# Other start addresses for matmul operands, another passage into the FFN, and twelve placements of FFN up's weights

## The chip, the core and the metric

The kernel runs on one core of one Trainium2 chip. The metric is device time in microseconds for one execution of the whole layer. The work of the five engines is named as the profile names it: PE is TensorE's matmuls and PEld its weight loads, DVE is VectorE, ACT is ScalarE, POOL is GpSimd, and SP is SyncE, which here only issues DMAs.

## What is computed

One layer of a diffusion backbone for 256 latent tokens and 256 context tokens of width 2048, all in fp32. Two token mixers (windowed attention with shared keys, neighbourhood attention) run in parallel, are gated, merged and projected; then comes a gated FFN with a short convolution:

```python
h = modulate(rms_norm(x, g_attn_pre), sh1, sc1)
hc = modulate(rms_norm(ctx, g_attn_pre), csh1, csc1)
# mixer: q, k, v, gates from h @ w_in (keys and values from hc too)
y = (sigmoid(ga) * (oa @ w_br_a) + sigmoid(gb) * (ob @ w_br_b)) @ w_o
x = x + gt1 * rms_norm(y, g_attn_post)

h = modulate(rms_norm(x, g_ffn_pre), sh2, sc2)
u = depthwise_conv(h @ w_up, conv_w, conv_b)       # 2048 -> 2 x 5632
a, g = split(u, 2)
x = x + gt2 * rms_norm((silu(g) * a) @ w_down, g_ffn_post)
```

The shifts, scales and gates come from `silu(c) @ w_mod + b_mod`.

## The kernel before

**Three matmuls for one product.** TensorE multiplies in a reduced form of fp32 here (`F32R`). So every operand is split in two parts, a high one (a rounded copy, made by ScalarE) and a low one (the rest, made by VectorE), in `split` (L114). A product is high x high + low x high + high x low; the low x low part is left out.

**Weights in blocks.** The weights `ws` come as 222 blocks of 128 x 2048 fp32 (1 MB), in the order in which they are used: values (10 blocks), queries (16), gates and branches (48), output projection (16), FFN up (88), FFN down (44); the constants `B_V` ... `B_DN` number the first of each. `raw_block` (L104) has SP load a block into one of four buffers `raw`; `halves` (L125) splits it in two halves of 1024 columns into the tiles `wh` and `wl` (two buffers each); `block` (L152) hands out the next one, has the one after it split, and loads some blocks ahead. The keys have units of their own (`ku`), in the buffers of `wh`.

**Two ways to use a block.** A matmul has a stationary operand, loaded by its weight load, and a moving one that streams past it.

- In the values (tile `pv`, L585), the output projection (`py_o`) and FFN down (`py_d`, both L800), the activations are stationary and the weights move, 512 columns at a time (the last part of the values: 256). Three matmuls make one product.
- In the queries (`pq`), gates (`pg`), branches (`pb`) and FFN up (`pu`), `mm2` (L159) has the weights stationary and the activations moving. The activations' high and low parts lie side by side, so one matmul with 512 columns does high and low against the high weights, and one with 256 columns does the low weights: a pair.
- The keys (`pk`, L387) have the weights stationary and 256 moving columns; the scores (`s`, L681) have 512 columns and run in runs of up to six within the queries.

**Where operands start.** SBUF tiles lie one after another, in the order in which pools and tiles are made, each rounded up to 32 bytes. In the built program this gives, in bytes past a multiple of 64 (every slice that a matmul takes starts at a multiple of 512 within its tile):

| Stage | stationary | moving |
|---|---|---|
| keys `pk` | weights 32 | activations 0 |
| values `pv` | activations 0 | weights 32 |
| queries `pq`, gates `pg` | weights 32 | activations 0 |
| scores `s` | queries 0 | keys 0 |
| branches `pb` | weights 32 | attention output 32 |
| output projection `py_o` | gated sum 32 | weights 32 |
| FFN up `pu` | weights 32 | activations 0 |
| FFN down `py_d` | gated FFN 32 | weights 32 |

**The passage into the FFN.** `norm_gain` (L787) does the output projection in four column groups. In the last, the last three blocks are done for the first 128 tokens (t = 0) and then for the other 128 (t = 1), so that the norm of the first half can run beside the matmuls of the second. `close` (L804) squares a half on ScalarE and multiplies by the gain on VectorE; `residual` (L870) takes the root (`rstd_tok`, L834), adds to x (`x1`, four steps of 512 columns), squares the sum for the next norm and takes its root. FFN up's first block is split in between, behind the first half's close (L832), its two pieces queued behind a step of `residual` (L879). `scaled` (L886) multiplies both halves by their scale, half of the column groups on ScalarE. Then 33 filler matmuls (`keep_busy`, L899), and 32 transposes (`ptx`, L905), whose output in PSUM is read by VectorE or ScalarE into a temporary `h2t` (L912, L914), by ScalarE into the high part of `h2` (L915), and from both VectorE makes the low part (L916). FFN up's matmuls follow as pieces of `h2` come.

A scheduler sets each engine's order from the program's order, the dependencies and its costs; `issue_after` queues an instruction behind another one on its engine. All engines work through their queues in order.

## Time and profile before

| | us |
|---|---|
| median of 3 runs | 1532.22 (1531.57 to 1532.34) |
| the profiled execution | 1532.26 |
| its span, first to last instruction | 1530.5 |

The granted clock of TensorE over the span is 0.999. By stage, from the first to the last matmul that writes the stage's tile:

| Stage | from | to |
|---|---|---|
| keys `pk` | 10.3 | 163.8 |
| values `pv` | 158.0 | 275.2 |
| queries and attention `pq`, `s`, `po` | 275.0 | 440.5 |
| gates and branches `pg`, `pb` | 440.4 | 691.4 |
| output projection `py_o` | 691.2 | 780.8 |
| transposes `ptx` | 787.7 | 796.9 |
| FFN up `pu` | 791.6 | 1281.2 |
| FFN down `py_d` | 1281.0 | 1522.9 |

A row of the profile's groups reads: line, engine, operation, output <- inputs (buffer numbers left out), shape, count, then busy time and mean duration of one, then the engine's idle time before it and what ended that. A row of the timeline begins with the start and the duration in microseconds. A matmul's duration includes its filling and draining, which overlap with its neighbours'; how far apart two matmuls start is read from their starts.

### The profile page before, as it was taken

To read this page: it belongs to the slowest core of one execution; us is meant where nothing else is said; L and a number is where in the kernel's file an instruction comes from. 1 tells how busy PE (TensorE), PEld (TensorE's weight loads), DVE (VectorE), ACT (ScalarE), POOL (GpSimd) and SP (SyncE) were. 2 spreads that over 40 slices of the span, in tenths; PEclk is the share of its full clock that TensorE was granted. 3 is DMA by queue.
4 is the path that set the end of the run, shared out by engine and by line. 5 is a ranking of instruction groups with operands and counts; after the bars stand their busy time and mean duration, and the time that the engine had idled before them with its cause. 6 is when DMAs were issued, how large, how long until landed. Compare 5 with 4: busy or idle time off the path is not lost.

```text
span 1530.5 us, 22661 instructions
## 1 busy us (share of the span) xinstructions
PE 1512.7 (99%) x9062; PEld 1319.4 (86%) x9062; DVE 1131.6 (74%) x1670; ACT 784.7 (51%) x1277; POOL 1.7 (0%) x10
## 2 busy tenths in 40 slices
PE   8999999999999999999999999999999999999998
PEld 8988888899988888888888888888888888888886
DVE  3478798888888989887768887888788776444444
ACT  4332533676774445454467555555555555344342
POOL 0000000000000000000000000000000000000000
PEclk9999999999999999999999999999999999999999
DMA  9978778634458888888955666666666556555552
GB/s 348 385 269 330 287 287 330 256 111 131 139 199 332 320 325 330 336 321 318 376 203 202 248 226 242 245 233 223 242 242 240 198 193 248 220 192 193 192 192 83
DMA packets 59113, 382.19 MB, mean 250 GB/s; under 512 B 6528, under 2 KB 6912, under 8 KB 16768
## 3 DMA queue, kind: packets, MB, share of 16 engines
q1 hardware_dynamic: 58288, 379.68, 67.1%
q8 instruction: 71, 1.16, 0.3%
q10 hardware_dynamic: 720, 1.07, 0.2%
q14 instruction: 34, 0.28, 0.0%
HBM read 376.48 MB, written 4.24 MB: 249 GB/s over the span
## 4 chain that ended last, share of the span: by engine, by line
PE 96%; DVE 1%; ACT 1%; DMA 1%; issue 1%; DVEq 0%; ACTq 0%
PE pu L164 21%; PE py_d L800 16%; PE pu L165 11%; PE pv L585 7%; PE pg L164 7%; PE pk L387 6%; PE py_o L800 5%; PE pq L164 4%; PE pb L164 4%; PE pg L165 4%; PE pq L165 2%; PE pb L165 2%; PE po L711 2%; PE s L681 1%; PE pm L295 1%; PE pt L702 1%
## 5 line engine op out<-in xcount | busy, mean ns | idle before, releaser
L122 DVE TENSOR_TENSOR wl<-raw,wh 128x1024 fp32r<-128x1024 f32 x444 | 529.7, 1221 | 236.7 <-ACT wh L118 236.3
L118 ACT ACTIVATE wh<-raw 128x1024 fp32r<-128x1024 f32 x444 | 453.1, 1054 | 300.8 <-PE py_d L800 131.3
L164 PE MATMUL pu<-h,wh 128*128 128x512 f32 x1408 | 488.6, 390 | 0.1
L165 PE MATMUL pu<-h,wl 128*128 128x256 f32 x1408 | 397.0, 282 | 0.0
L164 PEld LDWEIGHTS pu<-h,wh 128*128 128x128 f32 x1408 | 264.4, 188 | 55.8 <-DVE h L916 0.3
L165 PEld LDWEIGHTS pu<-h,wl 128*128 128x128 f32 x1408 | 266.1, 189 | 0.0
L800 PE MATMUL py_d<-wh,ff 128*128 128x512 f32 x704 | 218.1, 391 | 0.0
L164 PE MATMUL pg<-hx,wh 128*128 128x512 f32 x464 | 161.5, 390 | 0.0
L800 PEld LDWEIGHTS py_d<-wh,ff 128*128 128x128 f32 x704 | 132.2, 188 | 27.9
L194 DVE SCALAR_TENSOR_TENSOR raw<-raw,crb 128x2048 f32<-128x2048 f32 x64 | 146.1, 2285 | 3.8 <-DMA raw<-in_wm_b_dram 3.1
L800 PE MATMUL py_d<-wl,ff 128*128 128x512 f32 x352 | 138.0, 392 | 0.0
L165 PE MATMUL pg<-hx,wl 128*128 128x256 f32 x464 | 130.8, 282 | 0.0
L387 PE MATMUL pk<-hx,ku 128*128 128x256 f32 x480 | 117.0, 286 | 1.8 <-DVE kT L453 1.7
L387 PE MATMUL pk<-hc,ku 128*128 128x256 f32 x480 | 114.1, 280 | 0.0
L169 ACT ACTIVATE half_u<-pu 128x256 f32<-128x256 f32 x88 | 33.5, 383 | 152.8 <-PE pu L165 152.8
L164 PE MATMUL pq<-hx,wh 128*128 128x512 f32 x304 | 108.2, 395 | 0.0
L164 PEld LDWEIGHTS pg<-hx,wh 128*128 128x128 f32 x464 | 87.1, 188 | 18.4
L387 PEld LDWEIGHTS pk<-hx,ku 128*128 128x128 f32 x480 | 90.2, 188 | 6.8 <-issue 4.5
L387 PEld LDWEIGHTS pk<-hc,ku 128*128 128x128 f32 x480 | 90.4, 188 | 0.7 <-issue 0.2
L164 PE MATMUL pb<-oab,wh 128*128 128x512 f32 x256 | 90.5, 394 | 0.0
L165 PEld LDWEIGHTS pg<-hx,wl 128*128 128x128 f32 x464 | 87.7, 189 | 0.0
L165 PE MATMUL pq<-hx,wl 128*128 128x256 f32 x304 | 85.5, 281 | 0.0
(181 smaller groups left out, 1942.5 us busy)
## 6 DMA issues: line engine op xcount, KB each, us to landing
raw<-in_ws_dram SPq DMA_DIRECT2D x222, 1024.0 KB, 4.9
raw<-in_wm_b_dram SPq DMA_DIRECT2D x64, 1024.0 KB, 5.1
raw<-in_wm_sc_dram SPq DMA_DIRECT2D x15, 1024.0 KB, 8.2
raw<-in_wm_sh_dram SPq DMA_DIRECT2D x16, 768.0 KB, 7.2
raw<-in_wkt_dram SPq DMA_DIRECT2D x10, 1024.0 KB, 5.2
crb<-sild SPq DMA_DIRECT2D x6, 1024.0 KB, 7.1
raw<-in_wk_dram SPq DMA_DIRECT2D x7, 768.0 KB, 9.0
sd<-in_wm_sd_dram SPq DMA_DIRECT2D x4, 1024.0 KB, 8.8
```

Source lines behind the costliest of these rows:

```text
L118: a_ = nc.scalar.activation(hi, src, AF.Copy)
L122: v_ = nc.vector.tensor_tensor(out=lo, in0=src, in1=hi, op=ALU.subtract)
L164: nc.tensor.matmul(pt[:, :], wh[:, w], a, start=first and i == 0, stop=False, skip_group_check=True)
L165: nc.tensor.matmul(pt[:, :S], wl[:, w], a[:, 0], start=False, stop=last and i == n - 1, skip_group_check=True)
L169: a_ = nc.scalar.activation(t[:], pt[:, S:], AF.Copy)
L194: nc.vector.scalar_tensor_tensor(out=r, in0=r, scalar=1.0, in1=row, op0=ALU.mult, op1=ALU.mult, accum_out=modx[:, j : j + 1])
L295: nc.tensor.matmul(pm[32 * j : 32 * j + 32, t * P : t * P + P], cc[:, q, :], rsc[k + t][:, q * P : q * P + P], start=q < 4, stop=q >= KT - ...
L387: nc.tensor.matmul(pk[:, v * S : v * S + S], wt[:, w], hh[v][:, k, a], start=k == 0 and a == 0 and wt is wh and v == 0, stop=k == KT - 1 a ...
L585: nc.tensor.matmul(pv[i][:, :nw], src[:, k, a, t0 : t0 + P], wt[:, w], start=k == 0 and q == 0, stop=k == KT - 1 and q == 2)
L681: nc.tensor.matmul(s_ps[:], qs[hd][:, a, qt * P : qt * P + P], k_[:], start=q == 0, stop=q == 2)
L711: nc.tensor.matmul(po[:, :S], v_[:, b], pTs[hd][:, b, a], start=b == 0 and q == 0, stop=b == 3 and q == 2)
L800: nc.tensor.matmul(py[t][:], act[:, k, a, t * P : t * P + P], wt[:, w], start=k == 0 and q == 0, stop=k == nk - 1 and q == 2)
```

## The change

It has three parts.

1. **Places.** The small tiles at the start of SBUF change their order and sizes, `cr` and `c2` go into tiles that exist anyway, and the buffers of `wh` and `wl` become 32 elements (128 bytes) longer. All activations now start at 0 bytes past a multiple of 64 (of 128 too), and so do the weights' buffers. Within its buffer a block's high and low part start at an offset, in elements of 4 bytes, that `offset` gives by stage: (0, 0) for values, output projection and FFN down, (8, 8), that is 32 bytes, for queries, gates, branches and the first four blocks of FFN up. The keys' units start at 8 as well.
2. **Twelve placements.** The other 84 blocks of FFN up take the twelve pairs of the table `UP`, seven blocks each.
3. **Passage.** FFN up's first block is split with the blocks before it, ahead of the first half's close. `residual` and `scaled` are rewritten, with another order and share between ScalarE and VectorE; the scalings of column group 3 and one more are ScalarE's. There are 26 fillers in place of 33, and the first piece of `h2` gets a second pair of transposes into a bank of its own (`ptx0b`), which VectorE reads, while ScalarE reads the first one.

The core of the diff:

```diff
+UP = ((0, 8), (8, 0), (4, 4), (0, 4), (4, 0), (4, 8), (8, 4), (12, 12), (2, 2), (16, 16), (8, 24), (24, 8))
...
-    def halves(r, pool=None, after=None):
+    def halves(r, off, pool=None, after=None):
         n = r.shape[-1]
         b = 1 if pool else 2
-        h = (pool or wp).tile([P, 2048], F32R, tag="wh", bufs=b, name=f"wh{nraw[0]}")
-        lo = (pool or wp).tile([P, 2048], F32R, tag="wl", bufs=b, name=f"wl{nraw[0]}")
+        h, lo = (
+            (pool or wp).tile([P, 2048 + 32], F32R, tag=f"w{q}", bufs=b, name=f"w{q}{nraw[0]}")[:, off[i] : off[i] + 2048]
+            for i, q in enumerate("hl"))
...
+    def offset(i):
+
+        if B_UP + 4 <= i < B_DN:
+            return UP[(i - B_UP - 4) // 7]
+        return (0, 0) if i < B_Q or B_WO <= i < B_UP or i >= B_DN else (8, 8)
...
-                parts[q] = halves(raws[q], place.get(q), queue.get(q))
+                parts[q] = halves(raws[q], offset(q - b0), place.get(q), queue.get(q))
...
-                h = wp.tile([P, 2048], F32R, tag="wh", bufs=2, name=f"ku{u}")
+                h = wp.tile([P, 2048 + 32], F32R, tag="wh", bufs=2, name=f"ku{u}")[:, 8 : 8 + 2048]
...
                 for g in range(n - lead, n):
-                    wts.append(block(3, g < n - 1))
+                    wts.append(block(3))
                     part(wts[-1], g, 0)
                 for t in range(2):
...
-                    close(t)
-                    done(t)
-                    if t == 0:
-                        split_to(nblk[0])
+                    close(t, after)
+                    after = done(t)
...
                 a_ = nc.scalar.activation(yg[:, t, cs], x1[:, t, cs], AF.Square, accum_out=ss[:, 1, t, c : c + 1])
-                if t == c == 0:
-                    queue[b0 + B_UP] = (a_.ins, v_.ins)
-            rstd_tok(ss[:, 1, t], r[:, 1, t : t + 1])
-            if t:
-                with tc.issue_after(closed[0]), tc.issue_after(v_.ins):
-                    scaled(0)
-                scaled(1)
...
+            if t == 0:
+                rstd_tok(ss[:, 1, t], r[:, 1, t : t + 1])
+                return a_.ins
+            else:
+                v_ = v_.ins
+                for c in range(3):
+                    with tc.issue_after(v_):
+                        v_ = scaled(0, c)
+                with tc.issue_after(v_):
+                    rstd_tok(ss[:, 1, t], r[:, 1, t : t + 1])
+                scaled(1, 0)
+                a_ = scaled(1, 1)
+                scaled(1, 2)
+                with tc.issue_after(a_):
+                    a_ = scaled(0, 3)
+                with tc.issue_after(a_):
+                    scaled(1, 3)
+                for q in range(2):
+                    sync.dma_start(out=x1d[:, q], in_=x1[:, q])
+
+        def scaled(t, c):
+            cs = slice(c * 512, c * 512 + 512)
+            if c == 3 or (t, c) == (1, 1):
+                return nc.scalar.activation(yg[:, t, cs], x1[:, t, cs], AF.Copy, scale=r[:, 1, t : t + 1]).ins
+            return nc.vector.tensor_scalar(
+                out=yg[:, t, cs], in0=x1[:, t, cs], scalar1=r[:, 1, t : t + 1], scalar2=None, op0=ALU.mult).ins
+
+        norm_gain(zz, KT, yg, grow, ss[:, 0], "o", 2, residual, beside)
         zs.close()
         pu = [acc(f"pu0_{i}") for i in range(4)]
-        keep_busy(33, "2")
+        keep_busy(26, "2")
...
-                    nc.vector.tensor_scalar(out=t_[:], in0=px, scalar1=g_, scalar2=s_, op0=ALU.mult, op1=ALU.add)
+                    nc.vector.tensor_scalar(out=t_[:], in0=px if j else pt0[:, :S], scalar1=g_, scalar2=s_, op0=ALU.mult, op1=ALU.add)
```

Also in it, and not shown: a fourth buffer for the attention's small statistics tile (`st`), and the wider tiles for `r`, `gr` and the warm-up of the root, which only move what lies behind them.

Outside the passage, and a few matmuls of FFN up's first blocks beside it, every engine's instructions stand in the same order as before. In the passage, ScalarE's order from the first half's close on was, before (`py_o3_0` and `py_o3_1` are the two halves' sums, `wh192` is FFN up's first block):

```order
L805 ACTIVATE yg_7006,ss_7008<-py_o3_0_7445 128x512
L838 ACTIVATE r_7009<-ss_7008,r_7009 128x1
L877 ACTIVATE yg_7006,ss_7008<-x1_7005 128x512
L118 ACTIVATE wh192_7551<-raw190_7485 128x1024
L877 ACTIVATE yg_7006,ss_7008<-x1_7005 128x512 x3
L118 ACTIVATE wh192_7551<-raw190_7485 128x1024
L838 ACTIVATE r_7009<-ss_7008,r_7009 128x1
L805 ACTIVATE yg_7006,ss_7008<-py_o3_1_7446 128x512
L838 ACTIVATE r_7009<-ss_7008,r_7009 128x1
L890 ACTIVATE yg_7006<-x1_7005,r_7009 128x512 x2
L877 ACTIVATE yg_7006,ss_7008<-x1_7005 128x512 x4
L838 ACTIVATE r_7009<-ss_7008,r_7009 128x1
```

And in the changed kernel (with its own line numbers; the block is `wh191` there):

```order
L126 ACTIVATE wh191_7534<-raw190_7488 128x1024 x2
L821 ACTIVATE yg_7010,ss_7012<-py_o3_0_7448 128x512
L852 ACTIVATE r_7013<-ss_7012,r_7013 128x1
L891 ACTIVATE yg_7010,ss_7012<-x1_7009 128x512 x4
L821 ACTIVATE yg_7010,ss_7012<-py_o3_1_7449 128x512
L852 ACTIVATE r_7013<-ss_7012,r_7013 128x1 x2
L891 ACTIVATE yg_7010,ss_7012<-x1_7009 128x512 x4
L852 ACTIVATE r_7013<-ss_7012,r_7013 128x1
L915 ACTIVATE yg_7010<-x1_7009,r_7013 128x512 x3
L945 ACTIVATE h2_7005<-ptx0_7657,modx_74,gcol_75 128x256
```

Both pieces of the split moved from between the first half's squares to ahead of its close, and the scalings moved behind the second half's squares.

VectorE, from the second half's gain to the first piece of `h2`, before:

```order
L806 TENSOR_TENSOR yg_7006<-py_o3_1_7446,grow_7007 128x512
L839 RECIPROCAL r_7009<-r_7009 128x1
L874 SCALAR_TENSOR_TENSOR x1_7005<-yg_7006,r_7009,x1_7005 128x512 x4
L892 TENSOR_SCALAR yg_7006<-x1_7005,r_7009 128x512
L836 TENSOR_REDUCE r_7009<-ss_7008 128x1
L892 TENSOR_SCALAR yg_7006<-x1_7005,r_7009 128x512
L837 TENSOR_SCALAR r_7009<-r_7009 128x1
L839 RECIPROCAL r_7009<-r_7009 128x1
L892 TENSOR_SCALAR yg_7006<-x1_7005,r_7009 128x512 x2
L914 TENSOR_SCALAR h2t0_7665<-ptx0_7660,gcol_72,modx_71 128x256
L916 TENSOR_TENSOR h2_7001<-h2t0_7665,h2_7001 128x256
```

And in the changed kernel:

```order
L822 TENSOR_TENSOR yg_7010<-py_o3_1_7449,grow_7011 128x512
L853 RECIPROCAL r_7013<-r_7013 128x1 x2
L888 SCALAR_TENSOR_TENSOR x1_7009<-yg_7010,r_7013,x1_7009 128x512 x4
L916 TENSOR_SCALAR yg_7010<-x1_7009,r_7013 128x512 x3
L850 TENSOR_REDUCE r_7013<-ss_7012 128x1
L851 TENSOR_SCALAR r_7013<-r_7013 128x1
L853 RECIPROCAL r_7013<-r_7013 128x1
L916 TENSOR_SCALAR yg_7010<-x1_7009,r_7013 128x512 x2
L944 TENSOR_SCALAR h2t0_7664<-ptx0b_7656,gcol_75,modx_74 128x256
L946 TENSOR_TENSOR h2_7005<-h2t0_7664,h2_7005 128x256
```

Three scalings of the first half now stand ahead of the second half's reduce, where one stood before, and the first temporary is read from `ptx0b`.

66 lines of the change are left out of this document (32 added, 34 removed).

## The prediction

> **What bounds the kernel now.** I read the busy time on the page first, then the chain that ended last, then the timeline of TensorE inside each stage, and last the timeline around the passage from the output projection to FFN up.
>
> ```profile
> span 1530.5 us, 22661 instructions
> PE 1512.7 (99%) x9062; PEld 1319.4 (86%) x9062; DVE 1131.6 (74%) x1670; ACT 784.7 (51%) x1277; POOL 1.7 (0%) x10
> ...
> PE 96%; DVE 1%; ACT 1%; DMA 1%; issue 1%; DVEq 0%; ACTq 0%
> ```
>
> TensorE is busy for 99% of the span and makes up 96% of the chain. So only two things can move the time: how far apart the matmuls of a stage follow each other (the pitch), and the few places where TensorE waits. Most of the change is about the first, the new passage into FFN up about the second.
>
> A matmul's duration in a row (390 ns and so on) overlaps the next one, so it doesn't give the pitch. The starts do. From five stages, the first and the last row of a steady stretch (the columns are start, duration, engine, line, operation, output<-inputs, shape, count):
>
> ```profile
> 200.28 0.40 PE L585 MATMUL pv<-wl,hx 128*128 128x512 f32 x1
> ...
> 205.88 0.40 PE L585 MATMUL pv<-wl,hx 128*128 128x512 f32 x1
> ```
>
> ```profile
> 1399.61 0.39 PE L800 MATMUL py_d<-wl,ff 128*128 128x512 f32 x1
> ...
> 1402.36 0.39 PE L800 MATMUL py_d<-wl,ff 128*128 128x512 f32 x1
> ```
>
> ```profile
> 340.47 1.09 PE L681 MATMUL s<-k,q 128*128 128x512 f32 x4
> ...
> 395.38 1.54 PE L681 MATMUL s<-k,q 128*128 128x512 f32 x6
> ```
>
> ```profile
> 559.75 0.40 PE L164 MATMUL pb<-oab,wh 128*128 128x512 f32 x1
> ...
> 562.91 0.40 PE L164 MATMUL pg<-hx,wh 128*128 128x512 f32 x1
> ```
>
> ```profile
> 999.78 0.39 PE L164 MATMUL pu<-h,wh 128*128 128x512 f32 x1
> ...
> 1003.94 0.39 PE L164 MATMUL pu<-h,wh 128*128 128x512 f32 x1
> ```
>
> ```profile
> 59.77 0.28 PE L387 MATMUL pk<-hx,ku 128*128 128x256 f32 x1
> ...
> 61.87 0.28 PE L387 MATMUL pk<-hx,ku 128*128 128x256 f32 x1
> ```
>
> The same shape does not cost the same everywhere. With 512 moving columns: pv does 24 matmuls in 5.60 us, 0.2333 each; py_d 12 in 2.75 us, 0.2292; s, two more matmuls in a run cost 1.54 - 1.09 = 0.45 us, so 0.225 to 0.230 within the rounding of the rows, and I use 0.227. A pair of 512 and 256 columns takes 3.16/9 = 0.3511 in pb and 4.16/12 = 0.3467 in pu. The 256-column matmuls of pk follow at 2.10/18 = 0.1167. No row of these stretches has a wait behind it, and the granted clock is 1.00 (in the windows further down), so something about the operands makes the difference.
>
> Set beside the table of places in the section on the kernel, it sorts like this. Where the moving operand starts on a multiple of 64 bytes (s, pu, pk), the pitch is low. Where it starts 32 bytes past one (pv, py_d, pb), it is high, and highest in pv, where the stationary operand does not share that shift. That is a reading of six stages, not a shown cause; every term below that rests on it has a rival.
>
> **The change part by part.** All terms are against the profiled execution's own 1532.26 us (span 1530.5 and 1.76 around it), which is 0.04 above the median of 1532.22.
>
> *Places in FFN down, the output projection and the values.* Counts come from these rows:
>
> ```profile
> L800 PE MATMUL py_d<-wh,ff 128*128 128x512 f32 x704 | 218.1, 391 | 0.0
> L800 PE MATMUL py_d<-wl,ff 128*128 128x512 f32 x352 | 138.0, 392 | 0.0
> L800 PE MATMUL py_o<-wh,zz 128*128 128x512 f32 x256 | 79.0, 392 | 0.0
> L800 PE MATMUL py_o<-wl,zz 128*128 128x512 f32 x128 | 49.6, 393 | 0.0
> L585 PE MATMUL pv<-wh,hx 128*128 128x512 f32 x128 | 40.2, 396 | 0.5 <-ACT wh L118 0.5
> L585 PE MATMUL pv<-wl,hc 128*128 128x512 f32 x64 | 25.3, 395 | 0.0
> ```
>
> After the change both operands of these stages start on a multiple of 64, as in s, which has the same shape and the same rhythm of three matmuls (high by high, low by high, high by low). py_d and py_o together are 1440 matmuls: 1440 x (0.2292 - 0.227) = 3.2 us saved; with s at 0.225 it would be 6.0, with 0.230 a loss of 1.2. pv has two groups of 128 and two of 64, so 384 at 512 columns: 384 x (0.2333 - 0.227) = 2.4 saved (1.3 to 3.2). Its 192 matmuls of 256 columns I leave at nothing; half of pv's difference either way would be 0.6 us.
>
> *Places in the branches.* pb's 256 pairs get an aligned moving operand and a stationary one at 32, which is what pu has: 256 x (0.3511 - 0.3467) = 1.1 us saved. The queries and gates keep the relation that they have now, 32 for the weights and 0 for the activations, so nothing; the first four blocks of FFN up too. VectorE has slack for the faster pace: in the values it is the most loaded, and yet it is idle for a tenth.
>
> ```profile
> 160.00:270.00 110.00, 110.00 (x563) 92.71 (x562) 98.98 (x112) 45.32 (x77) 0.00 (x0) 1.00 0.78 296
> 792.00:1281.00 489.00, 489.00 (x2825) 433.28 (x2824) 388.85 (x579) 286.99 (x459) 0.00 (x0) 1.00 0.63 224
> ```
>
> (The columns after the stretch and its length are busy time and count of PE, PEld, DVE, ACT and POOL, then the granted clock, the DMA share and GB/s.) In the first row VectorE is busy 98.98 of 110 us, and the pace rises by 2.7%; in FFN up it is busy 388.85 of 489, so its splits, 128x1024 each, could take a quarter longer at odd addresses before it became the bound.
>
> *Twelve placements in FFN up.* 84 blocks of 16 pairs, in groups of 7 blocks or 112 pairs. The activations stay aligned. Counted past a multiple of 64, groups 11 and 12 have both parts at 32, as now: nothing. The other ten groups, 1120 pairs, stand at 0, 8, 16 or 48 bytes or in mixtures, which no stage of before shows. Bounds from rows: at the low end a pair made of s's 0.227 and pk's 0.1167, which is 0.3437, so 1120 x 0.0030 = 3.4 us saved; near by on the high side pb's 0.3511, so 1120 x 0.0044 = 4.9 lost; far out, both matmuls paying what pv pays over s, 2 x 0.0063, so 14.1 lost. The nearest rows are pu itself (all the activations' places and some of the weights' stay as they are there) and pb; I take half of pb's surcharge, 2.5 us lost.
>
> *The passage.* The rows around it, from the timeline (in brackets, the idle time before and what ended it), with a row of VectorE's splits from the page (busy time, mean ns) ahead of them:
>
> ```profile
> L122 DVE TENSOR_TENSOR wl<-raw,wh 128x1024 fp32r<-128x1024 f32 x444 | 529.7, 1221 | 236.7 <-ACT wh L118 236.3
> ```
>
> ```profile
> 775.74 0.60 ACT L805 ACTIVATE yg<-py_o 128x512 f32<-128x512 f32 x1 [7.82 <-PE py_o L800]
> 778.68 1.05 ACT L118 ACTIVATE wh<-raw 128x1024 fp32r<-128x1024 f32 x1
> 780.40 0.39 PE L800 MATMUL py_o<-wl,zz 128*128 128x512 f32 x1
> 781.47 1.04 ACT L118 ACTIVATE wh<-raw 128x1024 fp32r<-128x1024 f32 x1
> 782.60 0.57 ACT L805 ACTIVATE yg<-py_o 128x512 f32<-128x512 f32 x1
> 784.53 2.74 DVE L874 SCALAR_TENSOR_TENSOR x<-yg,r,x 128x512 f32<-128x512 f32 x4
> 787.19 0.48 DVE L892 TENSOR_SCALAR yg<-x,r 128x512 f32<-128x512 f32 x1
> 787.72 0.90 PE L905 MATMUL ptx<-ident,yg 128*128 128x128 f32 x6 [0.90 <-DVE r L836]
> 788.61 0.17 DVE L839 RECIPROCAL r<-r 128x1 f32<-128x1 f32 x1 [0.42 <-ACT r L838]
> 788.81 1.33 ACT L890 ACTIVATE yg<-x,r 128x512 f32<-128x512 f32 x2 [0.23 <-DVE r L839]
> 788.81 0.88 DVE L892 TENSOR_SCALAR yg<-x,r 128x512 f32<-128x512 f32 x2
> 789.35 2.18 PE L905 MATMUL ptx<-ident,yg 128*128 128x128 f32 x18 [0.73 <-DVE yg L892]
> 790.52 0.56 ACT L915 ACTIVATE h<-ptx,modx,gcol 128x256 fp32r<-128x256 f32 x1 [0.38 <-DVE h2t L914]
> 791.12 0.42 DVE L916 TENSOR_TENSOR h<-h2t,h 128x256 fp32r<-128x256 f32 x1 [0.63 <-ACT h L915]
> 791.60 0.19 PEld L164 LDWEIGHTS pu<-h,wh 128*128 128x128 f32 x1 [0.30 <-DVE h L916]
> ```
>
> The last output projection ends at 780.79 (780.40 + 0.39), and FFN up starts at 791.60: 10.8 us in which TensorE does only filler and transposes. ScalarE takes up the second half's square (L805) at 782.60, 1.8 late, because two splits of FFN up's first block (1.05 and 1.04) stand ahead of it. The change splits that block earlier; ScalarE's row at 775.74 had been idle for 7.82 us, which is room for both, and VectorE's part, two of 1.22, fits as well. Then I step through the new order with the old durations: the square at 780.83, the second half's four residual steps (2.74) from 782.5 in place of 784.53, so 2.0 earlier, to 785.25. Now three scalings of the first half (0.48 each) go ahead of the second norm on VectorE, to 786.6, where before one did; the reduce, the root and the reciprocal follow, and the second half's scale is there at 787.4 in place of 788.78. Then ScalarE has three scalings ahead of its first piece of h2 in place of two (1.33 for two, so some 1.9 for three): the first piece starts at 789.3 (before: 790.52), and its wait for VectorE's copy (0.38) goes, because that copy reads a bank of its own. VectorE's subtraction ends at 790.35 and FFN up starts at 790.4: 1.2 us saved. What is late next is ScalarE: the third scaling, which isn't needed for the first block. Bounds: nothing, if the split of the block reaches into the first half's close, and 2.0, if the two losses on the way hide. All later pieces of h2 keep their order, so I take them as shifted by the same 1.2. The DMA queue keeps its order as well; the load that waited for the moved split's buffer can go up to the store of x1 ahead of it, and nothing waits for that load here. The two extra transposes stand in a wait. Seven fillers fewer and the later second half leave a gap of some 1.6 us on TensorE where gaps of 0.90 and 0.73 were; over those the clock stayed at 1.00:
>
> ```profile
> 781.00:792.00 11.00, 9.31 (x79) 8.55 (x78) 8.34 (x21) 9.71 (x23) 0.00 (x0) 1.00 0.70 275
> ```
>
> *Sum:* -3.2 - 2.4 - 1.1 + 2.5 - 1.2 = -5.4, so 1532.26 - 5.4 = 1526.9 us.
>
> **The rivals.**
>
> *Only the relation between the operands counts* (both shifted alike is as good as both aligned). For it: py_d, both at 32, is far below pv. Against it: s lies under py_d. Then FFN down and the output projection stay, pv falls to 0.2292 (1.6 saved), and with 1.1, 1.2 and +2.5 it is 1530.9.
>
> *FFN up finds a better place.* The low bound for the ten groups: -3.4 where I put +2.5, so 1521.0. For it: pk's 0.1167 shows that a 256-column matmul can follow faster than the 0.118 or so that pu leaves it. Against it: pu's pitch doesn't vary at all over 12 pairs, as if at a limit.
>
> *Place is nothing.* If stationary and moving reads can't hinder each other, only the passage counts: 1531.1. Against it stand the three pitches of one shape. The Trainium skill states this rule ("SBUF — State Buffer", section "Who interferes with whom"): TensorE has two independent SBUF read ports, one for the moving operand and one for weight loads, and waits on no one. By that rule the change of places would bring nothing and the time would be 1531.1; the trace speaks against it with 0.2333 and 0.2292 for one shape at one clock.
>
> *The passage gains nothing,* although the new order of the instructions is certain: the gap, or the earlier split, takes the 1.2 back. 1528.1.
>
> *Slower: odd starts in FFN up hurt every weight load.* A stationary block that starts 8, 16 or 48 bytes into a 64-byte stretch, or high and low parts that start differently, may break the steady rhythm of pu. At the far bound this costs 14.1, and the sum is 1532.26 - 7.9 + 14.1 = 1538.5. It decides once the ten groups lose over 7.9 us, 7 ns a pair on average, and shows as measurably slower from 11 us, 9.8 ns a pair. Against it: none of the stages lies more than 4.4 ns a pair from pu.
>
> **How the numbers follow.** A measurement of this kernel can tell about 0.2%, 3.1 us: under 1529.2 counts as faster, over 1535.3 as slower. Forecast (aligned moving operands run as s does, FFN up loses a little): 46%, mostly under 1529.2. Only the relation: 15%. A better place found: 14%. Place is nothing: 7%. No gain in the passage: 6%. Odd starts hurt: 12%. Faster takes most of the first, all of the third and most of the fifth, and a quarter of the second: 63%; slower is the last with its milder forms below the threshold set off by the forecast's upper tail: 11%; the rest, 26%, is within 0.2%. The range for 8 in 10 leaves out the far halves of the third and the last case: 1521.5 to 1534.0.
>
> **What would show it.** In the changed profile, py_d's and pv's starts should stand 0.227 apart and pb's pairs 0.3467. FFN up should show twelve stretches of seven blocks, each steady within itself, the last two at 0.3467; a stretch with another pitch names a placement. FFN up's first weight load should come 9.6 us after the end of the last py_o, with ScalarE's square of the second half within 0.1 us of that end. I am wrong if py_d stays at 0.2292, if the queries' and gates' pairs move away from 0.3467 (then a longer period than 64 bytes counts), or if TensorE begins to wait for VectorE's splits in FFN up.

## The result, and the profile after

| | us |
|---|---|
| before, 4 runs beside the changed kernel | 1532.09 (1531.57 to 1532.34) |
| changed, 4 runs | 1539.9 (1539.58 to 1539.98) |
| ratio | 1.0052, 95% interval 1.0037 to 1.0067 |

The changed kernel is 7.8 us slower, where 5.4 us faster was forecast. The head of its page and its chain answer to those of before:

```profile
span 1538.2 us, 22638 instructions
PE 1522.1 (99%) x9050; PEld 1316.3 (86%) x9050; DVE 1132.7 (74%) x1671; ACT 783.9 (51%) x1276; POOL 1.7 (0%) x10
...
PE 96%; DMA 1%; DVE 1%; ACT 1%; issue 1%; DVEq 0%; ACTq 0%
```

TensorE has the same share of the chain as before, and it is busy 9.4 us longer with the same kind of work. So the question is again how far apart matmuls start. From the first matmul of each stage to the first of the next, from the starts in both traces (the keys from the span's start; the output projection and FFN down to the end of their last matmul, so the passage is from the end of the last `py_o` to the first matmul of FFN up):

| Stage | before | after | change | forecast |
|---|---|---|---|---|
| keys | 158.04 | 158.56 | +0.5 | not priced |
| values | 116.98 | 116.02 | -1.0 | -2.4 |
| queries, attention | 165.33 | 166.53 | +1.2 | 0 |
| gates, branches | 250.87 | 253.14 | +2.3 | -1.1 |
| output projection | 89.57 | 90.04 | +0.5 | -3.2 with FFN down |
| passage | 10.80 | 9.33 | -1.5 | -1.2 |
| FFN up | 489.44 | 494.25 | +4.8 | +2.5 |
| FFN down | 241.88 | 243.19 | +1.3 | see above |
| the rest | 7.55 | 7.14 | -0.4 | 0 |
| span | 1530.48 | 1538.20 | +7.7 | -5.4 |

Where the loss sits shows when the trace is cut block by block. The windows of the changed kernel below hold two neighbouring blocks each of the values, the gates and FFN down (in a row: from and to, the length, then busy time and count of PE, PEld, DVE, ACT and POOL, the granted clock, the DMA share, GB/s; each window runs from the first matmul of its block to the first of the next):

```profile
207.51:218.41 10.90, 10.90 (x49) 9.01 (x48) 10.87 (x11) 4.50 (x8) 0.00 (x0) 1.00 0.75 275
218.41:229.60 11.19, 11.19 (x49) 9.01 (x48) 11.12 (x11) 3.48 (x6) 0.00 (x0) 1.00 0.76 288
441.12:446.71 5.59, 5.59 (x34) 4.88 (x33) 5.46 (x12) 5.59 (x17) 0.00 (x0) 1.00 0.81 290
446.71:452.36 5.65, 5.65 (x35) 4.92 (x33) 5.54 (x8) 3.42 (x7) 0.00 (x0) 1.00 0.59 210
1304.36:1309.95 5.59, 5.59 (x25) 4.50 (x24) 2.36 (x2) 2.01 (x3) 0.00 (x0) 1.00 1.02 426
1309.95:1315.40 5.45, 5.45 (x25) 4.51 (x24) 2.36 (x2) 2.00 (x3) 0.00 (x0) 1.00 0.66 238
```

Neighbouring blocks do not cost the same, at the same clock and with the same work: 24 matmuls of FFN down take 5.59 and 5.45 us, 48 of the values 10.90 and 11.19. All through these stages the two values take turns, as the blocks take turns in the two buffers of `wh` and `wl`. In the built program the buffers, now 8320 bytes long, stand at 256 and 384 (`wh`) and at 0 and 128 (`wl`) modulo 512. Before, with 8192 bytes, all four stood at 288. Modulo 64 the new ones all agree, which is how the prediction looked at them.

The twelve placements of FFN up, seven blocks (112 pairs) to a window:

```profile
817.15:856.24 39.09, 39.09 (x227) 34.21 (x225) 33.39 (x54) 25.96 (x43) 0.00 (x0) 1.00 0.57 211
856.24:895.37 39.13, 39.13 (x227) 34.27 (x225) 30.36 (x44) 22.32 (x36) 0.00 (x0) 1.00 0.63 219
895.37:934.39 39.02, 39.02 (x226) 34.31 (x225) 31.45 (x47) 21.69 (x34) 0.00 (x0) 1.00 0.67 243
934.39:973.54 39.15, 39.15 (x226) 34.22 (x225) 32.19 (x47) 22.50 (x36) 0.00 (x0) 1.00 0.67 241
973.54:1012.96 39.42, 39.42 (x227) 34.28 (x225) 31.57 (x46) 21.68 (x34) 0.00 (x0) 1.00 0.65 238
1012.96:1052.06 39.10, 39.10 (x226) 34.18 (x225) 30.28 (x44) 22.38 (x36) 0.00 (x0) 1.00 0.62 219
1052.06:1091.52 39.46, 39.46 (x226) 34.33 (x225) 31.52 (x47) 21.73 (x34) 0.00 (x0) 1.00 0.68 242
1091.52:1130.47 38.95, 38.95 (x226) 34.16 (x225) 32.19 (x47) 22.50 (x36) 0.00 (x0) 1.00 0.67 243
1130.47:1169.56 39.09, 39.09 (x227) 34.18 (x225) 31.56 (x46) 21.82 (x34) 0.00 (x0) 1.00 0.66 237
1169.56:1209.12 39.56, 39.56 (x227) 34.45 (x226) 30.28 (x46) 22.30 (x36) 0.00 (x0) 1.00 0.61 218
1209.12:1248.28 39.16, 39.16 (x226) 34.27 (x225) 27.78 (x43) 21.56 (x34) 0.00 (x0) 1.00 0.53 188
1248.28:1287.87 39.59, 39.59 (x227) 34.34 (x226) 28.33 (x43) 22.42 (x37) 0.00 (x0) 1.00 0.53 186
```

At before's 0.3467 a window would be 38.83 long. None is; the eighth, (12, 12), comes nearest. The last one, priced at nothing, is the longest, though one transpose (`ptg`) that stands in it takes some 0.1 us of that; without it the tenth, (16, 16), is. TensorE is busy for the whole of every window and VectorE is not (33.39 of 39.09 at the most), so TensorE does not wait for the splits.

The passage in the timeline (start, duration, engine, line, operation, output<-inputs, shape, count; in brackets the idle time before):

```profile
783.90 0.40 PE L813 MATMUL py_o<-wl,zz 128*128 128x512 f32 x1
784.33 0.60 ACT L821 ACTIVATE yg<-py_o 128x512 f32<-128x512 f32 x1
788.57 1.27 DVE L916 TENSOR_SCALAR yg<-x,r 128x512 f32<-128x512 f32 x3
792.57 0.55 ACT L945 ACTIVATE h<-ptx,modx,gcol 128x256 fp32r<-128x256 f32 x1
793.62 0.19 PEld L179 LDWEIGHTS pu<-h,wh 128*128 128x128 f32 x1 [0.21 <-DVE h L946]
```

The last output projection ends at 784.30, ScalarE's square of the second half follows 0.03 later (1.8 before), and FFN up's first weight load comes 9.32 us after that end, where it was 10.81.

### The profile page after: what moved, and what is told of

Read it like the earlier page. It is cut to its first block, busy times and chain, and to the rows that moved or that the text cites. A ratio compares the mean times of both kernels' runs of the same rounds, so it can differ in the third digit from the quotient of the medians.

```text
span 1538.2 us, 22638 instructions
## 1 busy us (share of the span) xinstructions
PE 1522.1 (99%) x9050; PEld 1316.3 (86%) x9050; DVE 1132.7 (74%) x1671; ACT 783.9 (51%) x1276; POOL 1.7 (0%) x10
## 4 chain that ended last, share of the span: by engine, by line
PE 96%; DMA 1%; DVE 1%; ACT 1%; issue 1%; DVEq 0%; ACTq 0%
PE pu L179 21%; PE py_d L813 16%; PE pu L180 11%; PE pv L600 7%; PE pg L179 7%; PE pk L401 6%; PE py_o L813 6%; PE pq L179 4%; PE pb L179 4%; PE pg L180 4%; PE pq L180 2%; PE pb L180 2%; PE po L726 1%; PE s L696 1%; PE pm L309 1%; PE pt L717 1%
## 5 line engine op out<-in xcount | busy, mean ns | idle before, releaser
L130 DVE TENSOR_TENSOR wl<-raw,wh 128x1024 fp32r<-128x1024 f32 x444 | 529.4, 1221 | 240.0 <-ACT wh L126 239.5
```

The lines of the kernel that those rows point to most:

```text
L130: v_ = nc.vector.tensor_tensor(out=lo, in0=src, in1=hi, op=ALU.subtract)
```

## The experiments

The theory after the two traces: what counts is how far the weights' start lies from the activations' start, over a longer stretch than 64 bytes. The rivals: the passage or the odd offsets themselves cost the time, or the buffer or its neighbours in memory do.

**1. The passage alone.** The kernel before, with the changed kernel's `norm_gain`, `residual`, `scaled`, fillers and transposes, and nothing of the places:

```diff
-                    wts.append(block(3, g < n - 1))
+                    wts.append(block(3))
...
-        keep_busy(33, "2")
+        keep_busy(26, "2")
```

> The kernel before with nothing but the new passage into FFN up; all places as before. If the places are what cost the time, the passage alone keeps what the changed kernel's trace shows of it (10.80 us to 9.34 us from the last output projection to FFN up): 1532.1 - 1.4 = 1530.7 us, and every other stage runs as before. The rival, that the new passage itself costs the later stages something (an earlier split, another order of the stores), gives 1538 to 1540.

Measured: 1530.52 us (1530.38 to 1530.9), ratio 0.999, interval 0.9981 to 0.9999. The passage takes 9.33 us as in the changed kernel, and every other stage is within 0.2 us of before. So the passage gains its 1.5 us, and the loss is all in the places.

**2. All of FFN up at (8, 8).**

```diff
-UP = ((0, 8), (8, 0), (4, 4), (0, 4), (4, 0), (4, 8), (8, 4), (12, 12), (2, 2), (16, 16), (8, 24), (24, 8))
+UP = ((8, 8),) * 12
```

> The changed kernel with all twelve placements at (8, 8), so that all of FFN up stands at 32 bytes past a multiple of 64 for the weights and 0 for the activations, as before. By the prediction's reading (only the place modulo 64 counts) a pair takes 0.3467 us as before, and the time is 1539.9 - 4.8 = 1535.1 us. If the place counts over a longer period (the two buffers of the weights now lie 128 bytes apart modulo 512), the blocks alternate between 0.3533 and 0.3512 as in the gates of the changed kernel: 1344 pairs x 5.6 ns over before, 7.5 where the twelve placements cost 4.8, so 1542.6 us.

Measured: 1541.99 us, ratio 1.0065 (1.0049 to 1.0082). Two neighbouring blocks of 16 pairs of this kernel:

```profile
817.23:822.83 5.60, 5.60 (x35) 4.89 (x33) 4.06 (x7) 3.65 (x6) 0.00 (x0) 1.00 0.55 193
822.83:828.48 5.65, 5.65 (x35) 4.91 (x33) 4.15 (x7) 4.83 (x8) 0.00 (x0) 1.00 0.35 148
```

Before, such a block took 5.55. Modulo 64 this is before's placement, and it is worse than the twelve: 496.0 us for FFN up against 494.25. So remainders modulo 64 don't decide, and FFN up is slow without the odd offsets too.

**3. One relation in the output projection and FFN down.** A block that gets the first buffer starts 32 elements (128 bytes) in, one that gets the second starts at 0. So in both buffers the high part starts at 384 and the low part at 128 modulo 512, and the activations stand at 384, the same modulo 256:

```diff
+        seat = (0, 32) if pool else ((32, 32), (0, 0))[nhalf[0] % 2]
+        nhalf[0] += not pool
+        off = off or seat
...
+        if B_WO <= i < B_UP or i >= B_DN:
+            return None
```

> The changed kernel, but in the output projection and FFN down the block in the buffer at 256 modulo 512 starts 32 elements later, so that every block's high part starts at 384 and its low part at 128, with the activations at 384: the relation that the better half of the blocks has already. If the relation over 256 or 512 bytes counts, all 1440 matmuls run at 0.2267 where half ran at 0.2336: 720 x 6.9 ns = 5.0 us saved, 1534.9 us. If only the place modulo 64 or 128 counts, or the buffer itself, nothing changes: 1539.9 us.

Measured: 1534.91 us (1534.68 to 1535.67); against before the ratio is 1.0018 (1.0009 to 1.0027). Two neighbouring blocks of FFN down:

```profile
1302.59:1308.03 5.44, 5.44 (x26) 4.50 (x24) 2.36 (x2) 2.01 (x3) 0.00 (x0) 1.00 1.01 423
1308.03:1313.47 5.44, 5.44 (x26) 4.50 (x24) 2.36 (x2) 2.01 (x3) 0.00 (x0) 1.00 0.73 265
```

The alternation is gone, at the value of the better half. The buffers are the same two as before the edit, so it isn't the buffer: it is the start within it.

**4. A map of places.** Only TensorE's two forms, over one tile of zeros: three matmuls of 512 columns for a product (the first form, `triple`), and pairs (`pair`). `rh` and `rl` are how many bytes the high and the low weights stand past the activations, `m` shifts both:

```diff
+    R = range(0, 512, 32)
+    for m in (0, 96):
+        for r in R:
+            triple(r, r, m)
...
+    for rh in R:
+        for rl in R:
+            pair(rh, rl, 0)
```

> Not the layer: zeros are written to the output, and TensorE alone runs short stretches of the kernel's two forms (three matmuls of 512 moving columns for a product; pairs of 512 and 256) over one tile, with the start of the weights stepped against the start of the activations, by 32 bytes over 512, and both shifted together. If the relation alone counts, threes run at 0.2267 us at a difference of 0 or 256 and at 0.233 to 0.234 at 128, pairs at 0.3467 at -32, and a common shift of 96 bytes changes nothing. If the start of the moving operand modulo 64 counts, no row of the unshifted part differs from another at steps of 64, and a shift of 32 does. If the other engines' reads of the memory are the cause, all rows are alike, since they are idle here.

Measured, a window for a stretch: 24 matmuls of the first form at 0, 64, 128 and 224, at 128 with both operands shifted by 96, then 8 pairs at (224, 224), at (64, 0) and at (64, 256):

```profile
23.92:29.37 5.45, 5.45 (x25) 4.51 (x24) 0.00 (x0) 5.45 (x4) 0.00 (x0) 1.00 0.00 0
34.97:40.48 5.51, 5.51 (x26) 4.51 (x24) 0.00 (x0) 0.00 (x0) 0.00 (x0) 1.00 0.00 0
46.09:51.69 5.60, 5.60 (x26) 4.51 (x24) 0.00 (x0) 0.00 (x0) 0.00 (x0) 1.00 0.00 0
62.91:68.50 5.59, 5.59 (x25) 4.51 (x24) 0.00 (x0) 0.00 (x0) 0.00 (x0) 1.00 0.00 0
135.30:140.90 5.60, 5.60 (x26) 4.51 (x24) 0.00 (x0) 0.00 (x0) 0.00 (x0) 1.00 0.00 0
802.33:805.11 2.78, 2.78 (x19) 2.46 (x18) 0.00 (x0) 0.00 (x0) 0.00 (x0) 1.00 0.00 0
558.94:561.66 2.72, 2.72 (x18) 2.41 (x17) 0.00 (x0) 0.00 (x0) 0.00 (x0) 1.00 0.00 0
581.29:584.09 2.80, 2.80 (x19) 2.46 (x17) 0.00 (x0) 0.00 (x0) 0.00 (x0) 1.00 0.00 0
```

VectorE is idle, ScalarE too from the second stretch on, and no DMA runs, yet the stretches differ as the layer's stages do. The steady pitch, worked out from the starts inside a stretch and averaged over whole repeats of its pattern, beside the layer's:

| weights past activations, modulo 256 | map, ns | in the layer |
|---|---|---|
| 512 columns, 0 | 226.7 | values, `py_o`, `py_d` after, every second block; `s` before |
| 512 columns, 64 | 228.9 | `py_o`, `py_d` before: 228.9 |
| 512 columns, 128 | 233.3 | values, `py_o`, `py_d` after, every other block |
| 512 columns, 224 (-32) | 233.3 | values before: 233.3 |
| pair, 224 (-32) | 346.7 | queries, gates, FFN up before: 346.7 |
| pair, 128 | 351.0 to 351.3 | branches before: 351.1 |
| pair, 160 and 32 | 350.0 and 353.3 | gates after: blocks of 5.60 and 5.65 us |

In the first form a difference of r + 256 gives the same as r for all eight r, within 0.1 ns, and the shift by 96 changes no row by more than 0.6 ns. So with the other engines idle, and with high and low weights at the same difference, the relation decides, and its period is 256 bytes. Three things did not fit: (64, 0) gave 340.0 and (64, 256) 350.0; the same pairs at (0, 0) gave 346.7 once and 353.3 another time; and in the first form with high and low weights at different places, (0, 128) gave 228.9 and (256, 384) 233.3.

**5. A second map, with other stretches ahead.**

```diff
+    for a, b in TRY:
+        for c, d in BEFORE:
+            pair(c % 512, d % 512, 0, 5)
+            pair(a % 512, b % 512, 0, 13)
```

> Again not the layer, zeros as output. The first map showed one lower pitch for pairs than any stage of the layer has, 0.3400 us, with the high weights 64 bytes and the low ones 0 past the activations modulo 256, but 0.3500 for what should be the same place (64 and 256). If a stretch's pitch depends only on the place, (64, 0), (64, 256) and (320, 256) all give 0.3400 after every one of eight other placements run ahead of them. If the rhythm in which a stretch begins decides too, some of the eight lead to 0.3400 and others to 0.350 or so. If 0.3400 comes from the weight load that goes on beside a 256-column stream wanting 64 bytes and the one beside a 512-column stream wanting 0, the keys' form (256 columns, all loads alike) gives 0.1133 at 64 and no lower at any other place.

Measured, steady ns a pair, by what ran ahead (bytes, `rh` and `rl`):

```
             (0,0) (64,64) (96,160) (32,480) (-32,-32) (320,32) (200,300) (128,128)
(64, 0)      340.0   350.0    340.0    340.0     353.3    340.0     350.0     350.0
(64, 256)    340.2   349.8    340.0    340.0     353.3    340.0     350.0     350.0
(64, 16)     346.8   346.7    340.0    340.0     346.7    340.0     346.7     346.7
(-32, -32)   346.8   346.7    346.7    346.7     346.7    346.7     346.8     346.7
```

(320, 256) goes with the first two rows. So the place alone doesn't set the pitch everywhere: at some places TensorE settles in one of two or three rhythms, chosen by how the stretch begins, at others always in the same. The keys' form (256 columns) was lowest at 64 with 113.3 ns, 116.6 to 120.3 at the fifteen other places, but in twelve repeats behind other stretches 64 gave 117.8.

**6. One place for all.** The weights' buffers 2112 elements long, 8448 = 33 x 256 bytes, and small pads, so that all four buffers agree modulo 256 and all activations agree with them (56 elements are 224 bytes, or -32 modulo 256). Then one offset per form holds for every block:

```diff
-            (pool or wp).tile([P, 2048 + 32], F32R, tag=f"w{q}", bufs=b, name=f"w{q}{nraw[0]}")[:, off[i] : off[i] + 2048]
+            (pool or wp).tile([P, 2048 + 64], F32R, tag=f"w{q}", bufs=b, name=f"w{q}{nraw[0]}")[:, off[i] : off[i] + 2048]
...
+        if i < B_Q or B_WO <= i < B_UP or i >= B_DN:
+            return 0, 0
+        return 56, 56
```

> The changed kernel with the weights' buffers 8448 bytes long, so that all four stand alike modulo 256, and with every stage's activations at one remainder too; weights at 0 against the activations in values, output projection and FFN down, at -32 for both parts in keys, queries, gates, branches and all of FFN up (the relation of before). If only the relation modulo 256 counts, it is before, 1532.1, less the passage alone (1.6), less 1440 x (228.9 - 226.7) ns = 3.2 in the output projection and FFN down, less 384 x 6.6 ns = 2.5 in the values, less 256 x 4.4 ns = 1.1 in the branches, and 0.3 more for the values' 256-column matmuls: 1524.0 us. If the order of residues modulo 512 or a buffer of its own counts too, it stays above 1527.

Measured: 1524.39 us (1524.07 to 1524.96), ratio 0.9951 (0.9935 to 0.9968); every engine's instructions stand in the changed kernel's order. Two neighbouring blocks of the values:

```profile
206.04:216.92 10.88, 10.88 (x50) 9.01 (x48) 10.85 (x11) 4.43 (x9) 0.00 (x0) 1.00 0.78 282
216.92:227.80 10.88, 10.88 (x50) 9.01 (x48) 10.85 (x9) 3.87 (x6) 0.00 (x0) 1.00 0.76 287
```

By stage: values 114.81, gates and branches 249.72, output projection 88.62, FFN up 489.38, FFN down 239.53. These are the sizes that the map gives for the places, to 0.5 us in the sum. The 0.3 us by which every other block of the values was longer in the changed kernel are gone.

**7. The twelve placements on that ground.**

```diff
+        if B_UP + 4 <= i < B_DN:
+            return UP[(i - B_UP - 4) // 7]
```

> The kernel with one place for all four buffers, and FFN up's 84 blocks in the twelve placements, now without the buffers' own 128 bytes between them: the twelve placements by themselves. By the rows of the first map and of the changed kernel, (0,8), (4,4), (0,4), (4,8), (12,12) stay at 0.3467, (8,0), (4,0), (8,4) lose 3 to 4 ns a pair, (2,2) 2, (16,16), (8,24), (24,8) 5.5 to 7: with 112 pairs each 3.6 us over the kernel with one place, 1528.0 us, and all seven blocks of a placement alike. If alternation of the buffers was what made the placements cost, FFN up stays within 1 us of the kernel with one place, 1524.4.

Measured: 1528.42 us (1527.8 to 1528.82), ratio 0.9974 (0.9964 to 0.9984). FFN up takes 493.32 us, 3.9 over the kernel with one place. Placements 1, 2, 8 and 12 of this kernel:

```profile
809.62:848.45 38.83, 38.83 (x227) 34.01 (x225) 33.34 (x54) 26.03 (x43) 0.00 (x0) 1.00 0.60 213
848.45:887.79 39.34, 39.34 (x227) 34.30 (x225) 30.40 (x45) 22.35 (x36) 0.00 (x0) 1.00 0.63 217
1083.05:1121.88 38.83, 38.83 (x226) 34.09 (x225) 32.18 (x47) 22.52 (x36) 0.00 (x0) 1.00 0.68 243
1240.09:1279.62 39.53, 39.53 (x228) 34.39 (x226) 28.34 (x43) 22.42 (x37) 0.00 (x0) 1.00 0.52 186
```

Five placements, (0, 8), (4, 4), (0, 4), (4, 8) and (12, 12), are as good as before's, within 0.1 ns a pair; (2, 2), (4, 0) and (8, 0) lose 2.2, 3.3 and 4.6 ns; (8, 4), (16, 16) and (8, 24) 6.6; (24, 8) some 5.4, when the 0.1 us of the transpose in its window is left out. So the placements cost something by themselves, and none gains. That (8, 0) and (8, 4) would lose 3 to 4 was a miss.

**8. Pairs at (64, 16), and 9. at (64, 0).** The offsets of queries, gates, branches and FFN up in elements; the second also has the keys at 64 and the values' last part at 192:

```diff
-        return 56, 56
+        return 16, 4
```

> As the one with one place, but in queries, gates, branches and FFN up the high weights at 64 and the low ones at 16 against the activations, where the second map showed 340.0 or 346.7 ns a pair, by what ran ahead. If a stage keeps the rhythm in which it starts, each stage is at the one or at the other: 2432 pairs x 6.7 ns = 16.2 us is the most, so 1507.8 to 1524.0 us, and never above. If every block finds its own rhythm, the blocks of a stage differ among each other. If the map's rhythm does not hold beside the other engines' work, all pairs stay at 346.7 or above.

```diff
+        if B_V + 8 <= i < B_Q:
+            return 48, 48
...
-        return 56, 56
+        return 16, 0
```

> As the one before, but the low weights at 0, where the second map showed 340.0, 350.0 or 353.3 ns a pair by what ran ahead; besides the keys at 64 (113.3 or 117.8 ns in the map, 116.7 before) and the values' 256-column matmuls at 192 (113.3 or 117.8, where 0 gives 120). With the three rhythms held by stage, between 1507 and 1540 us, and a stage whose pairs are at 350 or 353 loses 3.3 or 6.6 ns a pair against before. If one rhythm always wins once the stage runs, all four stages are at the same of the three.

Measured for (64, 16): 1515.73 us (1515.34 to 1515.96), ratio 0.9893 (0.9878 to 0.9908). Two blocks of the gates, then two of FFN up:

```profile
439.18:444.73 5.55, 5.55 (x34) 4.88 (x33) 5.45 (x12) 5.55 (x17) 0.00 (x0) 1.00 0.79 300
444.73:450.28 5.55, 5.55 (x34) 4.88 (x33) 5.33 (x7) 3.44 (x7) 0.00 (x0) 1.00 0.57 193
809.88:815.32 5.44, 5.44 (x35) 4.81 (x33) 3.88 (x6) 3.65 (x6) 0.00 (x0) 1.00 0.54 185
815.32:820.76 5.44, 5.44 (x35) 4.81 (x33) 4.11 (x7) 4.84 (x8) 0.00 (x0) 1.00 0.40 167
```

One placement, two pitches: 5.55 / 16 = 346.7 ns all through the gates, 5.44 / 16 = 340.0 for 84 of FFN up's 88 blocks. The first two are mixed with the waits for `h2`; the last two, behind a single 128-column transpose (`ptg`), are at 346.7. FFN up falls to 480.32 us.

Measured for (64, 0): median 1530.79 us, ratio 0.998 (0.9957 to 1.0003), but from 1514.7 to 1533.77 over ten runs, where before stayed within 1.3. In its profiled run FFN up is at 350.0 but for its first two and last two blocks, and the gates change twice. The rows at both places, first a weight load that waits for VectorE's split, then the one transpose that stands between two blocks:

```profile
449.80 0.19 PEld L177 LDWEIGHTS pg<-hx,wl 128*128 128x128 f32 x1 [0.42 <-DVE wl L124]
...
601.34 0.39 PE L176 MATMUL pg<-hx,wh 128*128 128x512 f32 x1
...
601.68 0.39 PE L176 MATMUL pg<-hx,wh 128*128 128x512 f32 x1
601.90 0.28 PE L177 MATMUL pg<-hx,wl 128*128 128x256 f32 x1
602.02 0.27 PE L230 MATMUL ptg<-ident,gr 128*16 128x128 f32 x1
602.04 0.47 PE L176 MATMUL pb<-oab,wh 128*128 128x512 f32 x1
...
602.83 0.40 PE L176 MATMUL pb<-oab,wh 128*128 128x512 f32 x1
...
603.54 0.40 PE L176 MATMUL pb<-oab,wh 128*128 128x512 f32 x1
```

Ahead of the wait the pairs of the gates take 350.0 ns, from there on 340.0. Ahead of the transpose a pair takes 601.68 - 601.34 = 0.34; behind it two take 603.54 - 602.83 = 0.71, and the rest of the stage stays at 353.3. Nothing about the places changed at either point. So a rhythm is handed on from block to block until something stands between, and both points are read from this one profile: no run takes the wait or the transpose out. Nor does such a thing always change the rhythm. In the four kernels with these blocks at (64, 16), the eighth experiment's and the next three, the same transpose leaves the rhythm as it was (346.7 in two, 340.0 in two), while the transpose in FFN up turns 340.0 into 346.7 in all four. The keys' part held: keys 156.15 us, 1.6 less than with one place.

**10 to 12. Setting the rhythm.** One gate block behind the attention at (96, 160), which led to 340.0 in the second map; the same without that block; and the same with it, but with the blocks that run among the attention's matmuls back at -32. All three keep the keys at 64 and the values' last part at 192. The last kernel's places (the first has them without the first two lines):

```diff
+        if B_Q <= i < B_BR + 3:
+            return 56, 56
+        if i == B_BR + 3:
+            return 24, 40
         if i < B_Q or B_WO <= i < B_UP or i >= B_DN:
             return 0, 0
         return 16, 4
```

> The pairs at (64, 16) again, with the keys at 64 and the values' 256-column matmuls at 192 as in the run with (64, 0), and with one block, the first gate behind the attention, at (96, 160): in the second map five pairs of that ahead of (64, 16) led to 340.0 ns. If the rhythm is handed from block to block until TensorE waits, gates and branches run at 340.0 where they ran at 346.7: 720 pairs x 6.7 ns = 4.8 us less than the 1515.7 of (64, 16), with 2.3 less in the keys and 0.5 in the values, 1508.1 us. If one block of another place sets nothing, gates stay at 346.7 and it is 1512.9.

> The run with the one block at (96, 160), without that block: all gates at (64, 16). If that block set the rhythm of gates and branches, they go back to 249.7 us (346.7 ns a pair) and the time to 1509.1 + 4.2 = 1513.3 us. If the keys' or values' new places had set it, gates stay at 245.5 and the time at 1509.1.

> The run with the one block at (96, 160), with the blocks that run among the attention's other matmuls (the queries, three gates) back at -32, where the rhythm is always the same: the stage takes 165.7 us as in the kernel with one place, not 167.1, and the time is 1509.1 - 1.4 = 1507.7 us. If the block at (96, 160) needs the attention's old rhythm ahead of it, gates and branches go to 249.7 us and the time to 1512.

Measured:

| | time | ratio to before (interval) | queries, attention | gates, branches | FFN up |
|---|---|---|---|---|---|
| with the block | 1509.08 | 0.9849 (0.9836 to 0.9863) | 167.07 | 245.50 | 480.34 |
| without it | 1513.74 | 0.9886 (0.9869 to 0.9902) | 165.97 | 249.72 | 480.34 |
| with it, attention at -32 | 1508.76 | 0.985 (0.9835 to 0.9864) | 165.69 | 245.14 | 480.31 |

In the last kernel, the block at (96, 160), the block behind it, and the two after that:

```profile
436.48:442.13 5.65, 5.65 (x34) 4.89 (x33) 5.46 (x12) 5.65 (x17) 0.00 (x0) 1.00 0.81 287
442.13:447.57 5.44, 5.44 (x34) 4.82 (x33) 4.79 (x5) 3.39 (x7) 0.00 (x0) 1.00 0.48 160
447.57:458.45 10.88, 10.88 (x66) 9.65 (x65) 10.64 (x18) 5.68 (x9) 0.00 (x0) 1.00 0.81 313
```

With the one block gates and branches run at 340.0, without it at 346.7, and that is the only edit between the first two rows: it sets the rhythm. Its time missed the 1508.1 by 1.0; its keys gave 1.3 us in place of the 2.3 expected. In its profile a weight load waits 0.39 us for VectorE's split, two blocks behind the one at (96, 160), and the rhythm stays at 340.0. The queries' stage came back to 165.69 as expected in the last one, though the median fell by 0.3 us only: the first kernel's runs spread over 2.5 us with its profile at the upper end. At (64, 16) that stage took 165.97 to 167.07 us in three profiles, at -32 165.68 to 165.99 in three (the seventh experiment's is the third). So -32 looks the steadier there, on few profiles, and the gain of 1.4 was an overestimate. The last kernel is 1.5% faster than before and 2.0% than the changed one (1508.76 / 1539.9).

## Why the prediction was wrong

**The step that failed** is the sorting of the six stages by place modulo 64: "Where the moving operand starts on a multiple of 64 bytes (s, pu, pk), the pitch is low." It fitted all six stages of before, and was not the cause. The three terms that rest on it were to save 6.7 us; these stages and the queries and gates, priced at nothing, lost 4.3 together. `s` and `py_d` differ because `s` has both operands at 384 modulo 512, difference 0, and `py_d` has 288 against 480, 64 modulo 256; that both of `py_d`'s operands stand 32 past a multiple of 64 has nothing to do with it. The table of places in the section on the kernel gave remainders modulo 64 only, and so hid the 128 bytes that the longer tiles put between the buffers. The forecast named a longer period itself as what would show it wrong (the queries' and gates' pairs moving away from 0.3467), but gave it no case and no time.

**Output projection and FFN down** (forecast -3.2, measured +1.8): half the blocks went from 64 to 0, as s, and gained; the other half went to 128 (233.3 ns for 228.9) and lost twice as much. With all at 0, the third and sixth experiments give what the step asked for: FFN down 239.53, output projection 88.62, together 3.3 less than before. The size 0.227 was right, the condition was not.

**Values** (-2.4, measured -1.0): the same, from a worse start, so half a gain was left. With one place it is -2.2.

**Branches, queries, gates** (-1.1, and nothing for the queries and gates, which "keep the relation that they have now"; measured +2.3 and +1.2): the queries and gates kept 32 and 0 modulo 64, but went from -32 to 32 and 160 modulo 256, from 346.7 to 353.3 and 350.0 by turns; the branches came to the same two places from 128, at 351.1, so they did not get the 346.7 of `pu`. The zero was taken as certain, so no case of the range had these stages slower than before.

**Twelve placements** (+2.5, measured +4.8): on one place they cost 3.9, so the sign was right. The size was luck: each of the ten groups was to lose half of pb's surcharge, 2.2 ns a pair, but five of them lose nothing and five 2.2 to 6.6, which happens to make about the same 2.5. "Groups 11 and 12 have both parts at 32, as now: nothing" was wrong: they lose 6.6 and 5.4 ns a pair, the other 1.3 us. In the changed kernel the two buffers, 128 bytes apart, make of each placement two; so laid out the twelve cost 4.8 us, and (8, 8) throughout, in the second experiment, 6.6.

**The passage** (-1.2, measured -1.5): right in mechanism, with ScalarE's square 0.03 us behind the last matmul. The second half's scale was ready a little sooner than stepped, 6.4 us after that end in place of 6.6.

**The rivals.** "Only the relation between the operands counts" was the right one in kind, but it was worked out modulo 64 too, so its 1530.9 missed. "Place is nothing" has fallen: in the map the pitch goes from 226.7 to 234.3 ns with nothing else running. The Trainium skill's rule ("SBUF — State Buffer", section "Who interferes with whom") gives TensorE two independent read ports, one for the moving operand and one for weight loads, and says that it never waits on anyone; the map speaks against taking from this that places cost nothing, since there the pitch follows the difference of just these two starts. "Odd starts hurt" came nearest in its number, 1538.5, by luck: it put 14.1 us on FFN up, which lost 4.8, and left savings elsewhere that did not come. Its mechanism fails too: (4, 4), odd by 16 bytes, costs nothing, (16, 16), a whole 64, costs 6.6 ns a pair.

**What stays open.** Why the period is 256 bytes, the runs don't show. These figures would fit a stream of 512 columns that wants the weight load beside it at 0 and one of 256 columns that wants it at 64: pairs reach 340.0 = 226.7 + 113.3 ns where their high load stands at 64 and their low one at 0 or 16. That is an inference; what speaks for it is that the keys' form was lowest at 64 in the second map, as it asks for, and against it that the twelve repeats at 64 took 117.8. Which rhythm a stage settles in was found by trial, but for the block at (96, 160), whose effect the second map had shown. What a wait or a transpose does to it stays open.

## What to carry to other kernels

When a matmul's pitch differs between stages at the same clock, compare the difference of its operands' start addresses modulo 256 for each buffer in rotation, not remainders of single addresses: lengthening a rotating tile by 128 bytes changed every second block. Make rotating tiles a multiple of 256 bytes long, bring threes of 512 columns to difference 0 (3.3 us of 331 here, in the output projection and FFN down), and measure a small map of the forms before trusting a pattern that fits a handful of stages. Where a place has several rhythms, take one of which none is slower than what you have, as (64, 16) here with 340.0 or 346.7 for 346.7, and look at all the runs before believing one profile.

## What had not been expected of the hardware

- The steady pitch of one shape depends on the difference of two start addresses with a period of 256 bytes: 226.7 to 234.3 ns for 512 columns, 340.0 to 354 for a pair, with the other engines idle as well as busy.
- At some differences there are several steady rhythms: 340.0, 350.0 and 353.3 ns at (64, 0). In one profile the rhythm changed behind a wait of 0.42 us and again behind one 128-column transpose, then for the rest of the stage, and ten runs of that kernel spread from 1514.7 to 1533.8 us.
- One block of 16 pairs at another place sets the rhythm of the whole stage behind it: gates and branches take 245.50 us with it and 249.72 without.
- VectorE's splits don't mind odd destinations: 1221 ns on average before and after.
